# A weighted sum over eight experts: eight tokens per partition and store, weights in one transfer, loads and stores on separate queues

## The chip, the cores and the metric

The kernel runs on one core of a Trainium2 chip. The metric is the device time of one execution in microseconds; the time before is 721.33 us, the median of three runs (721.21 to 722.09). The profile shows one execution with a span of 720.4 us.

## The reference

For each of 16 x 1024 = 16,384 tokens there are eight expert outputs of 512 floats and eight weights. The result is their weighted sum:

```python
batch, seq, n_experts, expert_dim = 16, 1024, 8, 512
weights = combine_weights[..., np.newaxis]
return np.sum(expert_outputs * weights, axis=2).astype(np.float32)
```

All of it is float32. The kernel must read 268.4 MB of expert outputs and 0.5 MB of weights and write 33.6 MB. Each byte that is read takes part in one multiply-add, so no input is used twice.

## The kernel before

The tokens are cut into 64 chunks of 256. Each of the 128 partitions holds J = 2 tokens that follow each other in memory, so a partition's part of a load is one run of 2 x 8 x 512 x 4 B = 32 KB, and the runs of all partitions together are 4 MB in one piece. A chunk's output is 128 runs of 4 KB.

**Loads and queues.** `issue_load(m)` (L52) takes an input tile and a weight tile from pools of four and issues the load of chunk m on the SP queue for even m and on the ACT queue for odd m (L56). The weights of the chunk, 8 KB, come by a separate transfer from the POOL queue (L60). The loads of the last two chunks are cut in two, one token each (L59). Loads are issued three chunks ahead (LA = 3); from chunk 4 on, a load must wait until VectorE is done with the chunk four before it.

**Products.** For each token, VectorE makes the first product with `tensor_scalar_mul` (L77) and then adds seven more, each with one `scalar_tensor_tensor` (L83), which multiplies by a weight and adds to the accumulator `acc`. The chunk's store (L92) goes on the queue that did not load the chunk: ACT for even n, SP for odd n. Output tiles come from a pool of four, so the first product of a chunk waits until the store four chunks earlier has landed.

**The last two chunks.** They are handled together after the loop. ScalarE makes the products of experts 4 to 7 in bf16 (L111), VectorE those of experts 0 to 3 (L116, L122), then VectorE adds the two halves (L130, L135, L138), and each token's half of the output is stored by itself on SP (L141).

**What sets the order.** Each engine's instructions run in the order in which the scheduler put them, and an engine's queue is in order too: a transfer that ACT issues stands among ACT's computing instructions. On ACT the table load and the first product of the tail (L111) stand ahead of the load of chunk 63 (L59).

In the changed kernel the corresponding lines are: loads L62 (whole chunk) and L72 (pieces), the first product L86 on ScalarE, the seven multiply-adds L98, stores L113, and the weights L128.

Of the kernel before, what the change touches and what calls it, by code (L numbers as in the profile page):

```python
# [1 line left out]

# [4 lines left out]


@with_exitstack  # L10
def kernel(
    ctx: ExitStack,
    tc: tile.TileContext,
    expert_outputs: bass.AP,
    combine_weights: bass.AP,
    out: bass.AP,
):
    nc = tc.nc
    fp32 = mybir.dt.float32
    bf16 = mybir.dt.bfloat16  # L20

    B, S, E, D = expert_outputs.shape
    T = B * S
    P = 128
    J = 2
    n_steps = T // (P * J)

    eo_blk = expert_outputs.rearrange("b s e d -> (b s) e d").rearrange(
        "(n p j) e d -> n p j e d", p=P, j=J
    )  # L30
    w_blk = combine_weights.rearrange("b s e -> (b s) e").rearrange(
        "(n p j) e -> n p j e", p=P, j=J
    )
    o_blk = out.rearrange("b s d -> (b s) d").rearrange(
        "(n p j) d -> n p j d", p=P, j=J
    )

    in_pool = ctx.enter_context(tc.tile_pool(name="in_pool", bufs=4))
    w_pool = ctx.enter_context(tc.tile_pool(name="w_pool", bufs=4))
    out_pool = ctx.enter_context(tc.tile_pool(name="out_pool", bufs=4))  # L40
    prod_pool = ctx.enter_context(tc.tile_pool(name="prod_pool", bufs=2))

    ES = E // 2
    K_TAIL = 2

    load_engines = [nc.sync, nc.scalar]

    LA = 3
    in_tiles: list[bass.AP | None] = [None] * n_steps
    w_tiles: list[bass.AP | None] = [None] * n_steps  # L50

    def issue_load(m: int) -> None:  # L52
        in_t = in_pool.tile([P, J, E, D], fp32, name="in_t")
        w_t = w_pool.tile([P, J, E], fp32, name="w_t")
        if m < n_steps - K_TAIL:
            load_engines[m % 2].dma_start(out=in_t, in_=eo_blk[m])  # L56
        else:
            for j in range(J):
                load_engines[m % 2].dma_start(out=in_t[:, j], in_=eo_blk[m, :, j])  # L59
        nc.gpsimd.dma_start(out=w_t, in_=w_blk[m])  # L60
        in_tiles[m] = in_t
        w_tiles[m] = w_t  # L62

    for m in range(min(LA, n_steps)):
        issue_load(m)

    for n in range(n_steps):
        if n + LA < n_steps:
            issue_load(n + LA)
        if n >= n_steps - K_TAIL:  # L70
            continue
        in_tile = in_tiles[n]  # L72
        w_tile = w_tiles[n]
        acc = out_pool.tile([P, J, D], fp32)

        for j in range(J):
            nc.vector.tensor_scalar_mul(  # L77
                out=acc[:, j, :],
                in0=in_tile[:, j, 0, :],
                scalar1=w_tile[:, j, 0:1],  # L80
            )
            for e in range(1, E):
                nc.vector.scalar_tensor_tensor(  # L83
                    out=acc[:, j, :],
                    in0=in_tile[:, j, e, :],
                    scalar=w_tile[:, j, e : e + 1],  # L86
                    in1=acc[:, j, :],
                    op0=mybir.AluOpType.mult,
                    op1=mybir.AluOpType.add,
                )  # L90

        load_engines[(n + 1) % 2].dma_start(out=o_blk[n], in_=acc)  # L92

    tail_steps = list(range(n_steps - K_TAIL, n_steps))
    tail_accs = {}
    tail_prods = {}
    for n in tail_steps:
        acc = out_pool.tile([P, J, D], fp32, name="acc")  # L98
        prods = prod_pool.tile([P, J, E - ES, D], bf16, name="prods")
        tail_accs[n] = acc  # L100
        tail_prods[n] = prods

    for j in range(J):
        for n in tail_steps:
            in_tile = in_tiles[n]
            w_tile = w_tiles[n]
            acc = tail_accs[n]
            prods = tail_prods[n]

            for e in range(ES, E):  # L110
                nc.scalar.mul(  # L111
                    out=prods[:, j, e - ES, :],
                    in_=in_tile[:, j, e, :],  # L113
                    mul=w_tile[:, j, e : e + 1],
                )
            nc.vector.tensor_scalar_mul(  # L116
                out=acc[:, j, :],
                in0=in_tile[:, j, 0, :],
                scalar1=w_tile[:, j, 0:1],
            )  # L120
            for e in range(1, ES):
                nc.vector.scalar_tensor_tensor(  # L122
                    out=acc[:, j, :],
                    in0=in_tile[:, j, e, :],
                    scalar=w_tile[:, j, e : e + 1],
                    in1=acc[:, j, :],
                    op0=mybir.AluOpType.mult,
                    op1=mybir.AluOpType.add,  # L128
                )
            nc.vector.tensor_add(  # L130
                out=prods[:, j, 0:2, :],
                in0=prods[:, j, 0:2, :],
                in1=prods[:, j, 2:4, :],
            )
            nc.vector.tensor_add(  # L135
                out=prods[:, j, 0, :], in0=prods[:, j, 0, :], in1=prods[:, j, 1, :]
            )
            nc.vector.tensor_add(  # L138
                out=acc[:, j, :], in0=acc[:, j, :], in1=prods[:, j, 0, :]
            )  # L140
            nc.sync.dma_start(out=o_blk[n, :, j], in_=acc[:, j, :])  # L141


# [1 line left out]
_INS = ['expert_outputs', 'combine_weights']  # L145
_OUTS = [((16, 1024, 512), 'float32')]


# [23 lines left out]
```

## Time and profile before

| what | value |
|---|---|
| span | 720.4 us |
| VectorE busy | 644.4 us in 1020 instructions |
| of it the multiply-adds, L83 | 868 x 743 ns by the records |
| first products, L77 | 124 x 482 ns |
| ScalarE busy | 11.4 us, all after 690 us |
| moved by the transfers | 302.63 MB, mean 420 GB/s |
| a load of 4 MB, issue to landing | 33.5 us (median) |
| a store of 512 KB, issue to landing | 33.5 us (median) |
| the last store of 256 KB, issue to landing | 3.0 us (median) |

The time of a row in the page is that of its records. Instructions on VectorE overlap a little, so 14 multiply-adds that are recorded at 743 ns each pass in 9.28 us. The time from issue to landing of a load is long because several loads are queued at once; it is not the time that a load takes when it is alone. The DMA rate of a slice is what all 16 transfer engines of the core moved in it.

### The profile page before, as it was taken

How to read it: one execution, taken by the hardware profiler on the slowest of the kernel's cores; microseconds unless marked ns; L12 is line 12 of the kernel's file. 1: busy time of each engine (PE TensorE's matmuls, PEld its weight loads, DVE VectorE, ACT ScalarE, POOL GpSimd, SP SyncE). 2: the span in 40 equal slices, each digit the busy share in tenths (PEclk: the TensorE clock that was granted, in tenths of full speed). 3: DMA queues.
4: the chain of work that ended last, by engine and by line, in shares of the span. 5: the costliest groups of instructions: out<-in, count | busy, mean ns of one | idle time of the engine just before them, and what ended most of it. 6: DMA issues, size and time to landing. Idle time of an engine off the chain costs nothing.

```text
span 720.4 us, 1532 instructions
## 1 busy us (share of the span) xinstructions
DVE 644.4 (89%) x1020; ACT 11.4 (2%) x17; POOL 35.8 (5%) x68
## 2 busy tenths in 40 slices
DVE  0799999999998999989998999989998999999977
ACT  0000000000000000000000000000000000000023
POOL 1000000000000000000000000000000000000000
DMA  9999999999999999999999999999999999999993
GB/s 380 437 416 451 427 426 430 427 424 439 443 431 426 426 423 431 438 436 434 431 423 426 435 430 442 432 424 427 430 429 432 442 431 428 430 425 428 433 359 120
DMA packets 21068, 302.63 MB, mean 420 GB/s; under 512 B 3136, under 2 KB 4160, under 8 KB 12608
## 3 DMA queue, kind: packets, MB, share of 16 engines
q1 hardware_dynamic: 9792, 151.52, 49.2%
q10 hardware_dynamic: 9216, 150.47, 48.9%
q0 software_dynamic: 2048, 0.53, 0.3%
q14 instruction: 12, 0.10, 0.0%
HBM read 268.96 MB, written 33.55 MB: 420 GB/s over the span
## 4 chain that ended last, share of the span: by engine, by line
DMA 63%; DVE 35%; issue 1%; DVEq 0%; SPq 0%
DMA out_dram<-acc 56%; DVE acc L83 30%; DMA in_t<-in_expert_outputs_dram 8%; DVE acc L77 3%; DVE acc L122 1%; DVE acc L138 0%; DVE prods L130 0%; DVE acc L116 0%; DVE prods L135 0%; DVEq L77 0%; DVEq L116 0%; SPq L92 0%
## 5 line engine op out<-in xcount | busy, mean ns | idle before, releaser
L83 DVE SCALAR_TENSOR_TENSOR acc<-in_t,w_t,acc 128x512 f32<-128x512 f32 x868 | 580.1, 743 | 0.0
L77 DVE TENSOR_SCALAR acc<-in_t,w_t 128x512 f32<-128x512 f32 x124 | 54.6, 482 | 66.3 <-DMA in_t<-in_expert_outputs_dram 43.4
L60 POOL DMA_DIRECT2D w_t<-in_combine_weights_dram x64 | 35.6, 556 | 637.7 <-DVE acc L83 636.9
L111 ACT ACT_TABLE_LOAD x1 | 1.3, 1283 | 690.6 <-DMA in_t<-in_expert_outputs_dram 690.6
L111 ACT ACTIVATE prods<-in_t,w_t 128x512 bf16<-128x512 f32 x16 | 10.1, 709 | 9.0 <-DMA in_t<-in_expert_outputs_dram 9.0
L122 DVE SCALAR_TENSOR_TENSOR acc<-in_t,w_t,acc 128x512 f32<-128x512 f32 x12 | 8.9, 745 | 0.0
L116 DVE TENSOR_SCALAR acc<-in_t,w_t 128x512 f32<-128x512 f32 x4 | 1.9, 481 | 5.3 <-DMA out_dram<-acc 5.3
L138 DVE TENSOR_TENSOR acc<-acc,prods 128x512 f32<-128x512 f32 x4 | 2.8, 688 | 0.0
L130 DVE TENSOR_TENSOR prods<-prods 128x1024 bf16<-128x1024 bf16 x4 | 2.7, 683 | 0.0
L135 DVE TENSOR_TENSOR prods<-prods 128x512 bf16<-128x512 bf16 x4 | 1.7, 417 | 0.0
L156 POOL MEMSET const-float32-0.0<- 128x1 f32 x1 | 0.1, 99 | 0.2 <-issue 0.2
L156 POOL MEMSET const-bfloat16-1.0<- 128x1 bf16 x1 | 0.1, 102 | 0.0
L156 POOL MEMSET const-float32-1.0<- 128x1 f32 x1 | 0.1, 99 | 0.0
L156 POOL MEMSET const-uint8-127<- 128x1 uint8 x1 | 0.1, 99 | 0.0
## 6 DMA issues: line engine op xcount, KB each, us to landing
in_t<-in_expert_outputs_dram ACTq DMA_DIRECT2D x31, 4096.0 KB, 33.5
in_t<-in_expert_outputs_dram SPq DMA_DIRECT2D x31, 4096.0 KB, 33.3
out_dram<-acc ACTq DMA_DIRECT2D x31, 512.0 KB, 33.5
out_dram<-acc SPq DMA_DIRECT2D x31, 512.0 KB, 33.4
in_t<-in_expert_outputs_dram SPq DMA_DIRECT2D x2, 2048.0 KB, 31.2
in_t<-in_expert_outputs_dram ACTq DMA_DIRECT2D x2, 2048.0 KB, 13.9
w_t<-in_combine_weights_dram POOLq DMA_DIRECT2D x64, 8.0 KB, 6.9
out_dram<-acc SPq DMA_DIRECT2D x4, 256.0 KB, 3.0
```

Source lines behind the costliest of these rows:

```text
L60: nc.gpsimd.dma_start(out=w_t, in_=w_blk[m])
L77: nc.vector.tensor_scalar_mul(out=acc[:, j, :], in0=in_tile[:, j, 0, :], scalar1=w_tile[:, j, 0:1],)
L83: nc.vector.scalar_tensor_tensor(out=acc[:, j, :], in0=in_tile[:, j, e, :], scalar=w_tile[:, j, e : e + 1], in1=acc[:, j, :], op0=mybir.Al ...
L111: nc.scalar.mul(out=prods[:, j, e - ES, :], in_=in_tile[:, j, e, :], mul=w_tile[:, j, e : e + 1],)
L116: nc.vector.tensor_scalar_mul(out=acc[:, j, :], in0=in_tile[:, j, 0, :], scalar1=w_tile[:, j, 0:1],)
L122: nc.vector.scalar_tensor_tensor(out=acc[:, j, :], in0=in_tile[:, j, e, :], scalar=w_tile[:, j, e : e + 1], in1=acc[:, j, :], op0=mybir.Al ...
L130: nc.vector.tensor_add(out=prods[:, j, 0:2, :], in0=prods[:, j, 0:2, :], in1=prods[:, j, 2:4, :],)
L135: nc.vector.tensor_add(out=prods[:, j, 0, :], in0=prods[:, j, 0, :], in1=prods[:, j, 1, :])
L138: nc.vector.tensor_add(out=acc[:, j, :], in0=acc[:, j, :], in1=prods[:, j, 0, :])
L156: nc = _bacc.Bacc("TRN2", target_bir_lowering=False, num_devices=1)
```

## The change

The kernel is rewritten around the same arithmetic. Eight tokens that follow each other in memory now belong to one partition (K = 8). Loads still carry two tokens per partition (32 KB runs), but the runs of neighbouring partitions now lie 128 KB apart. The accumulator holds eight tokens, and one store writes 2 MB in runs of 16 KB for every four loads. All loads are issued by SP, four chunks ahead, into five buffers; the stores are issued by ACT, but for the last three. The weights of all tokens come in one transfer at the start, issued by ACT, with 16 runs of 256 B for each partition. ScalarE makes the first product of each token and writes it into the accumulator; VectorE adds the other seven. The last seven chunks are loaded in pieces, which get smaller towards the end, so that work on the last data can start before all of it is there. The last stores are smaller, too. The bf16 products of the last two chunks are gone.

The aim is to make the transfers' runs longer and fewer, to take work off VectorE and the POOL queue, to keep loads from standing behind stores or computing instructions, and to shorten the stretch between the last load and the end.

```diff
-    J = 2
-    n_steps = T // (P * J)
+    K = 8
+    G = 8
+    J = 2
+    N = T // (P * K)
...
-    in_pool = ctx.enter_context(tc.tile_pool(name="in_pool", bufs=4))
-    w_pool = ctx.enter_context(tc.tile_pool(name="w_pool", bufs=4))
-    out_pool = ctx.enter_context(tc.tile_pool(name="out_pool", bufs=4))
-    prod_pool = ctx.enter_context(tc.tile_pool(name="prod_pool", bufs=2))
+    in_pool = ctx.enter_context(tc.tile_pool(name="in_pool", bufs=5))
+    w_pool = ctx.enter_context(tc.tile_pool(name="w_pool", bufs=1))
+    out_pool = ctx.enter_context(tc.tile_pool(name="out_pool", bufs=2))
...
+    w_t = w_pool.tile([P, N, K, E], fp32, name="w_t")
+    chunks = [(n, k) for n in range(N) for k in range(0, K, J)]
+    last = len(chunks) - 1
...
+    def load(i):
+        n, k = chunks[i]
+        t = in_pool.tile([P, J, E, D], fp32, name="in_t")
+        in_tiles[i] = t
+        src = x[n, :, k : k + J]
+        if i < last - 6:
+            nc.sync.dma_start(out=t, in_=src)
+            return
+        for j in range(J):
+            if i == last and j == J - 1:
+                cuts = (0, 2, 4, 5, 6, 7, 8)
+            elif i >= last - 2:
+                cuts = (0, 4, 8)
+            else:
+                cuts = (0, 8)
+            for a, b in zip(cuts, cuts[1:]):
+                nc.sync.dma_start(out=t[:, j, a:b], in_=src[:, j, a:b])
...
+    def first(i):
...
+                nc.scalar.mul(
+                    out=acc[:, a + j],
+                    in_=in_tiles[i][:, j, 0],
+                    mul=w_t[:, n, k + j, 0:1],
+                )
...
+    def rest(i):
...
+            for e in range(1, E):
+                nc.vector.scalar_tensor_tensor(
+                    out=acc[:, a + j],
+                    in0=in_tiles[i][:, j, e],
+                    scalar=w_t[:, n, k + j, e : e + 1],
+                    in1=acc[:, a + j],
...
+    def store(i):
...
+        if i < last - 3:
+            if a == G - J:
+                put(nc.scalar, 0, G)
+        elif a == 2:
+            put(nc.scalar, 0, 4)
+        elif a == 4:
+            put(nc.sync, 4, 6)
+        elif a == 6:
+            put(nc.sync, 6, 7)
+            put(nc.sync, 7, 8)
...
+    AHEAD = 4
+    load(0)
+    nc.scalar.dma_start(out=w_t.rearrange("p n k e -> p n (k e)"), in_=w)
+    for i in range(1, AHEAD):
+        load(i)
+    first(0)
+    for i in range(len(chunks)):
+        if i + AHEAD <= last:
+            load(i + AHEAD)
+        if i < last:
+            first(i + 1)
+        rest(i)
+        store(i)
```

More of the change, by code (lines that the diff above doesn't have):

```diff
@@ L19 @@
     fp32 = mybir.dt.float32
-    bf16 = mybir.dt.bfloat16
+    mult, add = mybir.AluOpType.mult, mybir.AluOpType.add
     B, S, E, D = expert_outputs.shape
@@ L24 @@
     P = 128
+    K = 8
+    G = 8
     J = 2
-    n_steps = T // (P * J)
-    eo_blk = expert_outputs.rearrange("b s e d -> (b s) e d").rearrange(
-        "(n p j) e d -> n p j e d", p=P, j=J
-    )
-    w_blk = combine_weights.rearrange("b s e -> (b s) e").rearrange(
-        "(n p j) e -> n p j e", p=P, j=J
-    )
-    o_blk = out.rearrange("b s d -> (b s) d").rearrange(
-        "(n p j) d -> n p j d", p=P, j=J
-    )
-    in_pool = ctx.enter_context(tc.tile_pool(name="in_pool", bufs=4))
-    w_pool = ctx.enter_context(tc.tile_pool(name="w_pool", bufs=4))
@@ L40 @@
-    out_pool = ctx.enter_context(tc.tile_pool(name="out_pool", bufs=4))
-    prod_pool = ctx.enter_context(tc.tile_pool(name="prod_pool", bufs=2))
[L43 to L74, printed above, removed]
-        for j in range(J):
[L77 to L80, printed above, removed]
-            )
+    N = T // (P * K)
@@ new lines @@
+    x = expert_outputs.rearrange("b s e d -> (b s) e d").rearrange(
+        "(n p k) e d -> n p k e d", p=P, k=K
+    )
+    w = combine_weights.rearrange("b s e -> (b s) e").rearrange(
+        "(n p k) e -> p n (k e)", p=P, k=K
+    )
+    o = out.rearrange("b s d -> (b s) d").rearrange("(n p k) d -> n p k d", p=P, k=K)
+    in_pool = ctx.enter_context(tc.tile_pool(name="in_pool", bufs=5))
+    w_pool = ctx.enter_context(tc.tile_pool(name="w_pool", bufs=1))
+    out_pool = ctx.enter_context(tc.tile_pool(name="out_pool", bufs=2))
@@ new lines @@
+    w_t = w_pool.tile([P, N, K, E], fp32, name="w_t")
+    chunks = [(n, k) for n in range(N) for k in range(0, K, J)]
+    last = len(chunks) - 1
+    in_tiles = {}
+    accs = {}
+    pin = tc.keep_in_program_order
+    def load(i):
[6 more added lines that the diff above has]
+            return
+        for j in range(J):
+            if i == last and j == J - 1:
[6 more added lines that the diff above has]
+                nc.sync.dma_start(out=t[:, j, a:b], in_=src[:, j, a:b])
@@ new lines, in acc_of @@
+    def acc_of(i):
+        n, k = chunks[i]
+        g = (n, k // G)
+        if g not in accs:
+            accs[g] = out_pool.tile([P, G, D], fp32, name="acc")
+        return accs[g], k % G
+    def first(i):
+        n, k = chunks[i]
+        acc, a = acc_of(i)
+        for j in range(J):
+            pin(
+                nc.scalar.mul(
[3 more added lines that the diff above has]
+                )
+            )
@@ L82 @@
+    def rest(i):
+        n, k = chunks[i]
+        acc, a = acc_of(i)
+        for j in range(J):
             for e in range(1, E):
                 nc.vector.scalar_tensor_tensor(
[L84 to L89, printed above, removed]
-                )
-        load_engines[(n + 1) % 2].dma_start(out=o_blk[n], in_=acc)
@@ L94 @@
[L94 to L141, printed above, removed]
@@ new lines, in rest, with put @@
+                    out=acc[:, a + j],
+                    in0=in_tiles[i][:, j, e],
+                    scalar=w_t[:, n, k + j, e : e + 1],
+                    in1=acc[:, a + j],
+                    op0=mult,
+                    op1=add,
+                )
+    def store(i):
+        n, k = chunks[i]
+        acc, a = acc_of(i)
+        k0 = k - a
+        def put(queue, lo, hi):
+            pin(queue.dma_start(out=o[n, :, k0 + lo : k0 + hi], in_=acc[:, lo:hi]))
+        if i < last - 3:
[8 more added lines that the diff above has]
+            put(nc.sync, 7, 8)
```

## The prediction

> **What bounds the kernel now.** I read the page's 40 slices first, then the waits, the stretches, and last the end of the timeline. On the page, the rows of busy time, of DMA rate and of queues:
>
> ```profile
> DVE 644.4 (89%) x1020; ACT 11.4 (2%) x17; POOL 35.8 (5%) x68
> ...
> GB/s 380 437 416 451 427 426 430 427 424 439 443 431 426 426 423 431 438 436 434 431 423 426 435 430 442 432 424 427 430 429 432 442 431 428 430 425 428 433 359 120
> ...
> q1 hardware_dynamic: 9792, 151.52, 49.2%
> q10 hardware_dynamic: 9216, 150.47, 48.9%
> ```
>
> VectorE looks busiest, but the rate is flat from the second slice to the 38th, and the shares of the queues sum to 98.4% of all 16 DMA engines. Which of the two paces the other is told by VectorE's waits:
>
> ```profile
> DVE acc L77 <- DMA in_t<-in_expert_outputs_dram: 43.4, 25, 22.9
> DVE acc L77 <- DMA out_dram<-acc: 22.9, 24, 1.9
> ```
>
> 22.9 of the 43.4 us is the first load. The rest are about 1 us each, every chunk from 154 us on: VectorE needs 10.07 us a chunk, the transfers more. The stretches (columns: busy us per engine, clock, DMA share, GB/s) show the same, and where it stops:
>
> ```profile
> 154.00:660.00 506.00, 464.93 (x734) 0.00 (x0) 24.79 (x46) 1.00 1.01 431
> 660.00:689.00 29.00, 26.69 (x44) 0.00 (x0) 1.07 (x2) 1.00 0.98 420
> 689.00:693.00 4.00, 4.00 (x7) 2.42 (x3) 0.00 (x0) 1.00 0.51 155
> 693.00:701.00 8.00, 4.47 (x8) 1.43 (x3) 0.00 (x0) 1.00 1.05 435
> 701.00:706.00 5.00, 3.20 (x6) 4.74 (x8) 0.00 (x0) 1.00 0.85 299
> 706.00:716.00 10.00, 9.97 (x18) 2.83 (x5) 0.00 (x0) 1.00 0.23 87
> ```
>
> So: transfers bound the kernel to 689 us; then a hole, the last 4 MB alone, and ten microseconds of VectorE with the transfers nearly idle. The timeline tells what made the hole:
>
> ```profile
> 690.57 1.28 ACT L111 ACT_TABLE_LOAD   x1 [690.57 <-DMA in_t<-in_expert_outputs_dram]
> 690.72 0.82 ACTq L59 DMA_DIRECT2D in_t<-in_expert_outputs_dram  x2
> ```
>
> The last loads stand on ACT's in-order queue behind the tail's first product, which waits for chunk 62's data. Their buffer had been free since about 673.5 us.
>
> **What the Trainium skill says.** "DMA: Bandwidth & Descriptors", Bandwidth: 16 ports give 435 GB/s. The trace agrees: 431 to 432. Same page, Queues, rings and completion order: each engine takes turns between queues, a packet at a time. The packet records agree: at 300 to 345 us each engine goes row by row, a 32 KB load row of one queue, a 4 KB store row of the other. Same page, Latency and other measured facts: a row pitch of 512 KiB costs copies between HBM tensors 3% (207 against 214 GB/s); no run here shows one.
>
> **The change, part by part.**
> Prices from the packet records (a row on one engine): 32 KB 1213 ns, 16 KB 611, 8 KB 309, 4 KB 159, 2 KB 85, 512 B 27, completion 9. The records overlap: the share is 1.01, and a chunk's records, 8 x (1213 + 159) + 54 = 11.03 us, pass in 10.96 (56 chunks between 52.4 and 666.3 us). So I multiply by 0.9935.
>
> 1. *Stores of 16 KB rows, no weight packets per chunk.* Per chunk now 8 x 1213 + 2 x 611 + 11 = 10.94 us recorded, x 0.9935 = 10.87, against 10.96: 0.09 x 64 = 6 us less, all on the path.
> 2. *Loads on one queue.* Between 684 and 689 us one queue alone carried 430 to 432 GB/s, so one is enough. Five buffers keep 4 loads queued; a VectorE chunk (below) is shorter than a load, so buffers come free in time. Cost nothing.
> 3. *First product on ScalarE.* 128 VectorE instructions go. 14 multiply-adds pass in 9.28 us, 0.663 each: 896 x 0.663 = 594 us, 9.3 a chunk. ScalarE adds 2 x 0.71 us a chunk (row L111, which writes bf16; at twice that it would still hide), beside VectorE. Both hide under 10.87. On ACT's queue a 2 MB store stands behind the next chunk's product and so waits for that chunk's load, some 2 us; its buffer is wanted 4 chunks later. The store waits at L77 (22.9 us) go, but that is time VectorE had to spare.
> 4. *Tail.* The loads stay on SP, so the hole of about 3 us goes. Transfers to the last landing: loads 57 x 8 x 1213 + 8 x 8 x 611 + 10 x 8 x 309 + 2 x 8 x 159 + 4 x 8 x 85 ns = 622.1 us; stores but for the last 1 MB, 15 x 8 x 611 + 8 x 309 = 75.8; weights 2.3 (step 5); completions 0.9. Sum 701.1, x 0.9935 = 696.6. Before, two loads (19.3 us) and the first weights were in at 22.3, so the start costs 2.6: 699.2. One engine lags: near 666 us the last of a load's 16 completions comes 6.8 us after the first, the 15th only 0.8. That engine also carries the 8 KB instruction fetches (queue q14; 11 by then), 0.6 us each. With some 1130 instructions instead of 1532 I take 8 to 9: 5.2 us. **Last landing: 704.4.** The last token's final seven multiply-adds start after the token before: its second half lands 4.8 us before the end (2 MB at 431), seen 0.6 later, 4 x 0.663, then 7 x 0.663: VectorE ends 3.1 after the last landing. Before, VectorE ended at 716.05 and the span at 720.4: 4.35 for store and end. 704.4 + 3.1 + 4.35 = 711.9; the median lay 0.9 above the span: **712.8 us**.
> 5. *Weights in one transfer on ACT's queue.* 2048 runs of 256 B, 128 an engine. Trace of before: no such rows. A row's records fit 8.4 ns plus its bytes at 27.2 GB/s: 18 ns each, 2.3 us; upper end 60 ns (7.7 us), from the 85 of a 2 KB row. The cost is not the work but the turn. Behind it on ACT's queue: the table load (1.28 us) and the first product, which all of VectorE waits for. If one packet holds 16 runs, as the 4 KB that a partition receives, the weights need 8 turns beside load rows, some 12 us, in by 16: VectorE starts near 18, frees its first buffer near 27, and the five loads issued at once last to 51. Nothing lost.
>
> **The rivals.**
> *A: no stall, as summed, 712.8.*
> *B: a packet is one run.* Then each run waits for a 32 KB row: the five loads (40 rows an engine, 48 us) pass with only 40 of 128 runs, to 51.5. The other 88 take 1.6 to 5.3 us, then 1 of completion, 1.3 table load, 0.8 product, 9.3 VectorE for chunk 0, and 1.2 from issue to the first packet: transfers resume at 66.7 to 70.4. Idle beyond the runs' own time: 13.6 to 17.3 us. **728 us**, slower than before. For it: the 2 KB store rows at L141 are separate records, and the turns go strictly row by row. Against: queue q0's weight packets hold eight 64 B rows each (512 B), so a packet of several runs exists here; and the page names 9 to 17 descriptors a packet as typical. Five or more runs a packet are enough to escape.
> *C: the new pitch hurts.* Rows of a load now lie 128 KB apart instead of 32. At 1 to 3% of the transfers, 7 to 21 us: **720 to 734**. Against: the pitch is a quarter of the one that cost 3%.
> *D: the slow engine's lag vanishes* or records overlap more: 5 us less, **708**.
>
> **How the numbers follow.** A 61%, B 26%, C 6%, D 7%. The likeliest is A, 712.8. The range reaches from 709 (A with half the lag) to 730, which takes in B, and leaves out about 8% below and 8% above. Faster by over 0.2% (below 719.9): A, D and a little of C, 0.69. Within it: 0.04, from C. Slower: B and most of C, 0.27.
>
> **What would show it.** Steps 1 and 2: a rate of 432 to 433 in the middle and 10.9 us between chunks. Step 3: VectorE busy about 665 us by its records (896 x 743 ns), waiting for loads, never for stores. Step 4: no hole after 680, VectorE done some 3 us after the last load. Step 5: VectorE's first instruction near 18 us; B shows it past 55, with an idle slice near 55 to 67. C shows 32 KB rows over 1213 ns. The forecast is wrong if the weights land after about 38 us, or if the rate is under 428.

## The result, and the profile after

The changed kernel takes 733.06 us (median of four, 732.67 to 733.57) against 721.68 for the kernel before (four executions beside it), a ratio of 1.016 with a 95% interval of 1.0145 to 1.0174: 1.6% slower. The forecast was 712.8, with a range up to 730. Rival B told the mechanism; its 728 is 5 us short, because it stood on the same 712.8.

From the page of the changed kernel, the busy times, the 40 slices, ACT's queue (packets, MB, share) and the weights' transfer (last column: us from issue to landing):

```profile
DVE 603.8 (83%) x896; ACT 86.9 (12%) x129; POOL 0.2 (0%) x4
...
DVE  0009999999997969887897978969888897989998
...
DMA  9994999999999999999999999999999999999993
GB/s 381 429 366 190 400 420 430 432 432 431 436 429 435 431 431 430 436 436 420 440 426 438 430 432 431 435 429 434 432 434 426 438 431 433 424 429 429 425 416 142
...
q10 hardware_dynamic: 4368, 33.03, 10.7%
...
w_t<-in_combine_weights_dram ACTq DMA_DIRECT2D x1, 512.0 KB, 53.1
```

VectorE has three empty slices at the start (18.3 us each), and the transfers are weak in the fourth. The weights, 0.5 MB, need 53 us. The timeline of the start shows what hangs on them:

```profile
0.73 0.46 ACTq L128 DMA_DIRECT2D w_t<-in_combine_weights_dram  x1
...
12.94 1.28 ACT L86 ACT_TABLE_LOAD   x1 [12.94 <-DMA in_t<-in_expert_outputs_dram]
53.87 6.23 ACT L86 ACTIVATE acc<-in_t,w_t 128x512 f32<-128x512 f32 x10 [39.65 <-DMA w_t<-in_combine_weights_dram]
54.62 55.74 DVE L98 SCALAR_TENSOR_TENSOR acc<-in_t,w_t,acc 128x512 f32<-128x512 f32 x84 [54.62 <-ACT acc L86]
```

ScalarE waits 39.65 us for the weights, then makes ten products at once, because five chunks are there; VectorE's first instruction is at 54.6. The stretches (length; busy us of VectorE, ScalarE and POOL with their instructions; clock; DMA share; GB/s) tell what the transfers do meanwhile:

```profile
20.00:50.00 30.00, 0.00 (x0) 0.00 (x0) 0.00 (x0) 1.00 0.99 423
50.00:70.00 20.00, 15.38 (x24) 6.23 (x10) 0.00 (x0) 1.00 0.42 149
...
400.00:650.00 250.00, 213.12 (x320) 31.40 (x47) 0.00 (x0) 1.00 1.00 431
```

Up to 50 us they run at full rate and fill the five buffers. Then they have nowhere to put data until VectorE has used chunk 0. The packet records, each the time of one packet on one DMA engine, give the cause row by row: from 3.4 to 51.5 us each DMA engine does one 256 B run of the weights, one 32 KB load row, one run, and so on. I call this taking turns. At about 51.5 the load rows end; some 43 of an engine's 128 runs have passed, and the other 85 pass in less than 2 us, 14 to 25 ns apart. The next load row comes at about 65.

The middle is as fast as it was (431 GB/s). The end shows no hole. There VectorE is at work without a gap, so it no longer waits for loads (timeline of VectorE alone, the last 70 us):

```profile
658.11 70.20 DVE L98 SCALAR_TENSOR_TENSOR acc<-in_t,w_t,acc 128x512 f32<-128x512 f32 x93 [1.36 <-ACT acc L86]
```

93 instructions in 70.2 us are 0.755 each. In the middle they come 0.663 apart.

### The profile page after: what moved, and what is told of

It is laid out like the page before. It is cut to its first block, busy times and chain, and to the rows that moved or that the text cites. A ratio compares the mean times of both kernels' runs of the same rounds, so it can differ in the third digit from the quotient of the medians.

```text
span 731.4 us, 1345 instructions
## 1 busy us (share of the span) xinstructions
DVE 603.8 (83%) x896; ACT 86.9 (12%) x129; POOL 0.2 (0%) x4
## 3 DMA queue, kind: packets, MB, share of 16 engines
q10 hardware_dynamic: 4368, 33.03, 10.7%
## 4 chain that ended last, share of the span: by engine, by line
DMA 62%; DVE 29%; another core or an unknown queue 5%; issue 2%; ACT 1%; SPq 0%; ACTq 0%; DVEq 0%
DMA in_t<-in_expert_outputs_dram 62%; DVE acc L98 29%; ACT acc L86 1%; ACT L86 0%; SPq L72 0%; ACTq L86 0%; SPq L62 0%; DVEq L98 0%
## 5 line engine op out<-in xcount | busy, mean ns | idle before, releaser
L98 DVE SCALAR_TENSOR_TENSOR acc<-in_t,w_t,acc 128x512 f32<-128x512 f32 x896 | 603.8, 746 | 124.5 <-ACT acc L86 122.0
L86 ACT ACTIVATE acc<-in_t,w_t 128x512 f32<-128x512 f32 x128 | 85.6, 714 | 620.9 <-DMA in_t<-in_expert_outputs_dram 528.8
L86 ACT ACT_TABLE_LOAD x1 | 1.3, 1283 | 12.9 <-DMA in_t<-in_expert_outputs_dram 12.9
## 6 DMA issues: line engine op xcount, KB each, us to landing
w_t<-in_combine_weights_dram ACTq DMA_DIRECT2D x1, 512.0 KB, 53.1
```

Of the source, the lines that this page charges most:

```text
L86: nc.scalar.mul(out=acc[:, a + j], in_=in_tiles[i][:, j, 0], mul=w_t[:, n, k + j, 0:1],)
L98: nc.vector.scalar_tensor_tensor(out=acc[:, a + j], in0=in_tiles[i][:, j, e], scalar=w_t[:, n, k + j, e : e + 1], in1=acc[:, a + j], op0=mult,
```

## The experiments

Each time below is the median of 4 to 17 executions, which lie 0.2 to 2.2 us apart from lowest to highest. The ratio is to the kernel before, run beside it, with its 95% interval in brackets.

**The weights first.** The same transfer on the loads' queue, ahead of them:

```diff
-    load(0)
-    nc.scalar.dma_start(out=w_t.rearrange("p n k e -> p n (k e)"), in_=w)
+    nc.sync.dma_start(out=w_t.rearrange("p n k e -> p n (k e)"), in_=w)
+    load(0)
```

> The changed kernel with the same weight transfer issued on SP ahead of the first load, in place of ACT behind it; nothing else. Theory 1 (each 256 B run on ACT's queue waits its turn behind a 32 KB load row): ahead of the loads in one queue there are no turns, the 128 runs of an engine take 2.3 us (18 ns each), the weights land before 8 us, VectorE starts near 16 us, no idle slice near 53 to 65; 14 us less than the changed kernel, 718 to 721 us. Rival (the transfer of 2048 runs is slow by itself, some 50 us): the loads now stand behind it and the time rises above 760 us.

Measured: 719.05 us, ratio to the kernel before 0.9962 (0.9948 to 0.9977). The same 2048 runs now land 4.2 us after their issue. VectorE's start in the timeline:

```profile
17.60 22.61 DVE L98 SCALAR_TENSOR_TENSOR acc<-in_t,w_t,acc 128x512 f32<-128x512 f32 x34 [17.60 <-ACT acc L86]
```

14.0 us are gone with one moved line. The transfer is not slow by itself. This edit changes its queue and its place at once; the next two runs tell what made it slow.

**The weights from POOL.** The changed kernel with `nc.gpsimd` in place of `nc.scalar` in that line.

> The changed kernel with the weight transfer issued by POOL at the same place, behind the first load's issue; nothing else. Theory 1, that the number of packets counts and not the runs: queue q0 packed eight 64 B runs in a packet before; if it packs runs of 256 B too, an engine has 8 to 64 packets instead of 128, the weights land between 12 and 40 us, and with 8 to 28 packets the stall is gone: 719 to 721 us. If it sends one run a packet, the weights land near 53 us again and the time is 733 us. Rival (any transfer of this shape takes some 50 us beside loads): 733 us in every case.

Measured: 719.07 us, ratio 0.9964 (0.9951 to 0.9977). The page's queues, and the issue with its us to landing:

```profile
q10 hardware_dynamic: 2304, 32.51, 10.6%
q0 software_dynamic: 144, 0.52, 0.2%
...
w_t<-in_combine_weights_dram POOLq DMA_DIRECT2D x1, 512.0 KB, 17.7
```

Queue q0 carries the whole transfer in 128 packets of 4096 B and 16 completions: 16 runs a packet, eight packets an engine, each still with its turn beside a load row. ACT's queue had sent 2048 packets of 256 B (q10 falls from 4368 to 2304: 2048 runs and 16 completions). The weights are in at 18.9 us, and the time is that of the run with the weights first. So the packet counts, not the run, and the two queues pack differently.

**Three buffers.** The changed kernel, stall and all, with fewer loads issued at once.

```diff
-    in_pool = ctx.enter_context(tc.tile_pool(name="in_pool", bufs=5))
+    in_pool = ctx.enter_context(tc.tile_pool(name="in_pool", bufs=3))
...
-    AHEAD = 4
+    AHEAD = 2
```

> The changed kernel with three input buffers and loads two chunks ahead in place of five and four; the weight transfer stays on ACT behind the first load. Theory 1 (the runs take turns with whatever load rows are queued, and pass freely once the queue is empty): three loads are issued at once, 24 rows an engine, so the weights land near 2.6 + 29.3 + 2 = 34 us instead of 53, VectorE starts near 35, and the idle stretch of the transfers is as long as before, from about 34 to 46 us; the time stays at 731 to 735 us. Rival (the weights' landing near 53 is a property of their transfer): VectorE starts at 54 again, the transfers idle from 32 us, and the time rises to 750 us or more.

Measured: 732.9 us, ratio 1.0155 (1.0138 to 1.0171). VectorE's start, from the timeline, and one of the stretches:

```profile
35.23 35.20 DVE L98 SCALAR_TENSOR_TENSOR acc<-in_t,w_t,acc 128x512 f32<-128x512 f32 x53 [35.23 <-ACT acc L86]
```

```profile
34.00:46.00 12.00, 10.77 (x17) 3.78 (x6) 0.00 (x0) 1.00 0.13 38
```

The weights land when the queued load rows are through, here 24 an engine, at 34 us. From the last of the weights to the next load row it is 11.7 us, as in the changed kernel, and the time is the same. So the landing follows the number of load rows queued beside the weights, and the loss is what follows the landing (first product, chunk 0, the next issue).

**VectorE's order in the tail.** The multiply-adds of chunks 57 to 62 go in turns between the two tokens, as the scheduler has them in the middle; where loads are cut by token, it had put each token's seven in a row.

```diff
+        if last - 6 <= i < last:
+            pairs = [(j, e) for e in range(1, E) for j in range(J)]
```

> The changed kernel, with the multiply-adds of the chunks 57 to 62 in turns between the two tokens, as the scheduler has them in the chunks before; chunk 63 and all transfers unchanged, the weight stall stays. Theory 2 (in the tail each multiply-add waits for the one just before it on the same accumulator and takes 0.787 us instead of 0.663, so VectorE is the bound of the tail): spacing 0.66 us in these chunks, a chunk in 9.3 instead of 10.8 us, VectorE waits for loads again, 2 to 5 us less, 728 to 731 us. Rival (the last loads set the end, and VectorE's spacing is beside them): within 0.7 us of 733.1.

Measured: 732.9 us, ratio 1.0162 (1.0144 to 1.0179). No gain, the rival's number. The spacing did fall from 0.787 to 0.663 us, but in this order each chunk's second instruction waits for its second token.

**Both edits.**

> Both edits together: weights on SP ahead of the first load, and the chunks 57 to 62 in turns between the two tokens. If the two faults are independent, the gains add: 733.1 - 14 - 2 to 5, 714 to 717 us, near the 712.8 that was forecast without a stall. Rival (the tail's cost is only what the stall left behind): no less than the kernel with the weights first alone.

Measured: 719.27 us, ratio 0.9968 (0.9956 to 0.9979), the same as with the weights first alone. Missed again. VectorE waits for the second token of chunk 62 and then has 27 instructions left:

```profile
695.57 18.73 DVE L101 SCALAR_TENSOR_TENSOR acc<-in_t,w_t,acc 128x512 f32<-128x512 f32 x27 [0.58 <-ACT acc L86]
```

The last loads landed some 6 us later than forecast; the next run takes away a store that stands beside them.

**The last big store out of the loads' way.** With the weights first, the 1 MB store of chunks 60 and 61 moves to SP, behind all loads:

```diff
         elif a == 2:
-            put(nc.scalar, 0, 4)
+            put(nc.sync, 0, 4)
```

> Weights first (as in the run of that name), and the 1 MB store of chunks 60 and 61 on SP, where it stands behind all loads, instead of ACT, where its 8 KB rows take turns with the last loads. Theory 3 (the last landing on the slowest engine sets the end, and every store row that gets its turn before it moves it back): 1 MB less ahead of the last load, 2.4 us at 431 GB/s; VectorE ends 1.5 to 2.4 us earlier, 716.5 to 717.5 us. Rival (VectorE's chain of the last chunks, back to back from 640 us on, sets the end): within 0.7 us of 719.05.

Measured: 718.88 us, ratio 0.9961 (0.9947 to 0.9975). The last token's product started at 703.4 us, for 706.2 with the weights first alone, but VectorE had been busy without a gap and ended as late as ever:

```profile
643.94 70.20 DVE L98 SCALAR_TENSOR_TENSOR acc<-in_t,w_t,acc 128x512 f32<-128x512 f32 x93 [1.35 <-ACT acc L86]
```

The same 93 instructions, the same 70.20 us as in the changed kernel: moving loads forward does nothing for them.

**Both tail edits, with the weights first.**

> Weights first, the multiply-adds of chunks 57 to 62 in turns between the two tokens, and the 1 MB store of chunks 60 and 61 on SP behind the loads. Theory 5 (the tail has two limits of the same length: VectorE's chain at 0.787 us an instruction, and the last loads that share turns with store rows; taking away one alone leaves the other): both gone, the last loads land 2 to 3 us earlier and VectorE is free to follow, 714 to 716.5 us. Rival (something else sets the end, such as the lag of one DMA engine): within 0.7 us of 719.

Measured: 718.64 us, ratio 0.9962 (0.995 to 0.9975). Missed: VectorE was free of its chain, but the same 27 instructions stand at the end:

```profile
696.78 18.72 DVE L101 SCALAR_TENSOR_TENSOR acc<-in_t,w_t,acc 128x512 f32<-128x512 f32 x27 [0.57 <-ACT acc L86]
```

In this order chunk 62 can begin in earnest only when its second token is there. Its 13 remaining instructions and the 14 of chunk 63 then need until 715.5 (the profiled execution is the slowest of the five, 720.36 us). So this edit did not take VectorE's limit away; it put another one of VectorE in its place. A further run was to put the second token's first instructions of the last chunk between the first token's:

> As the run with turns and stores, and in the last chunk too the second token's first multiply-adds stand between those of the first token. Theory 5: VectorE has some 1 us less to do after the last landing, 0.5 to 1.5 us less than that run. Rival (VectorE waits for the last pieces, not for itself): no difference above 0.4 us.

Measured: 719.03 us, ratio 0.9964 (0.9951 to 0.9976). The scheduler already had the last chunk in that order (the waits of the last 16 instructions are the same in both traces), so this is the same instruction order twice. It shows that 0.4 us between two medians here mean nothing.

**Tokens in a pipeline.** As with both tail edits, but from chunk 60 on a token's last three multiply-adds stand between the first four of the next, across chunks.

```diff
+        for j in range(J):
+            old = left.pop() if left else None
+            for e in range(1, 5):
+                step(i, j, e)
+                if old and e < 4:
+                    step(*old, e + 4)
+            left.append((i, j))
```

> As the run with turns and stores (718.64), but in chunks 60 to 63 the last three multiply-adds of a token stand between the first four of the next token, across chunks: no instruction waits for the one just before it, and none waits for a token that it does not need. Theory 6 (VectorE sets the end of the tail, by its order: chained it needs 5.4 us a token where a token lands every 4.9, and in turns inside a chunk it starts only at the chunk's second token): VectorE ends some 7 us after the last token's first piece instead of 10.8, 2 to 3.5 us less, 715 to 716.5 us. Rival (the lag of the DMA engine with VectorE's fetches sets the end whatever the order): within 0.7 us of 718.6.

Measured: 717.96 us, ratio 0.9944 (0.9931 to 0.9958), the lowest median of the complete kernels. It gained 0.7 us where 2 to 3.5 were expected, which by the medians is the rival's result. The timeline speaks for the order all the same:

```profile
701.79 11.73 DVE L98 SCALAR_TENSOR_TENSOR acc<-in_t,w_t,acc 128x512 f32<-128x512 f32 x17 [0.24 <-ACT acc L86]
```

VectorE ends 8.8 us after the last token's product starts, for 10.8 with both tail edits, if not the 7 expected. The product starts at 704.7 in both profiled executions, and these took 718.35 and 720.36 us, 2.0 apart. Five executions of each leave open whether the gain is nearer to 0.7 or to 2.

**Less work on VectorE.** As with the last stores on SP, but two of the seven multiply-adds are left out in chunks 57 to 63, so the output lacks two products there.

```diff
-            for e in range(1, E):
+            for e in range(1, E if i < last - 6 else E - 2):
```

> As the run with the last stores on SP (718.88), with the multiply-adds of experts 6 and 7 left out in chunks 57 to 63 (2 of 7 for 14 tokens a partition; the output lacks them), all transfers unchanged. Theory 6: five chained multiply-adds take 3.9 us a token, less than the 4.9 in which a token lands, so VectorE follows the loads and the end is the last landing, near 707, plus 1 to 3 us and the last store: 711 to 714 us. Rival (the loads or the lag set the end): within 0.7 us of 718.9.

Measured: 714.63 us, ratio 0.9907 (0.9894 to 0.9921), 4.25 less than the run it builds on; the expected 711 to 714 was missed by 0.6. VectorE waits between tokens now:

```profile
690.16 3.90 DVE L98 SCALAR_TENSOR_TENSOR acc<-in_t,w_t,acc 128x512 f32<-128x512 f32 x5 [0.52 <-ACT acc L86]
695.13 3.90 DVE L98 SCALAR_TENSOR_TENSOR acc<-in_t,w_t,acc 128x512 f32<-128x512 f32 x5 [1.07 <-ACT acc L86]
700.10 7.71 DVE L98 SCALAR_TENSOR_TENSOR acc<-in_t,w_t,acc 128x512 f32<-128x512 f32 x10 [1.07 <-ACT acc L86]
```

With the transfers unchanged and less work, the end moves: VectorE's work bounded the tail. Seven chained instructions need 5.4 us a token where one lands every 4.9 to 5.0; five need 3.9. VectorE itself ends 6.3 us earlier, at 707.8; the last store now lands 4.0 us after its issue instead of 2.0, with the three stores ahead of it landing at 709.3 to 711.2.

**The lagging DMA engine.** Two kernels with instructions that nobody waits for. With the weights first, 1024 memsets on POOL:

> Weights first, and 1024 memsets of one element a partition on POOL, which has nothing else to do; nobody waits for them. Theory 4 (each 8 KB instruction fetch costs one DMA engine about 0.96 us, 0.31 for itself and 0.65 more on the row behind it, and the lagging engine sets every landing): 1024 instructions of 64 B are 8 more fetches, all on the same engine, the lag near 640 us grows from 7 to about 15 us, and the time rises by 6 to 8 us to 725 to 727 us. Rival (the lag is hidden by what the other engines do, or the fetches spread): within 0.7 us of 719.05.

Measured: 718.80 us, ratio 0.9959 (0.9944 to 0.9974). Eight more fetches are in the records, but the time did not move. In the spread of a load's 16 completions near 514 us, the last is 5.3 us behind the first and the 15th 5.1; without the memsets it is 5.2 and 1.5. So a second engine seems to lag beside the first one, and no further than it. Which engine carries which fetch the records do not name; this spread is the evidence.

Then 512 memsets on VectorE, added to the kernel with both tail edits:

> As the run with turns and stores, and 512 memsets of one element a partition on VectorE, near the start, where VectorE has time to spare later on; nobody waits for them. Theory 4b (POOL's fetches fell on another DMA engine than VectorE's, and the end is set by the engine that carries VectorE's fetches, some 0.9 us each): 4 more fetches on that engine, its lag near 640 us grows by 3 to 4 us, and the time by 2.5 to 4 us. Rival (the lag is hidden): within 0.7 us of the run with turns and stores.

Measured: 722.72 us, ratio 1.0017 (1.001 to 1.0024), 4.1 us more than the run it builds on (3.1 between the two profiled executions). The page has 14 fetches for 10:

```profile
q14 instruction: 14, 0.11, 0.0%
```

Near 534 us the last completion is 10.6 us behind the first instead of 7.4 (6.2 with the weights first alone), while the first one comes at the same time, 534.0 for 534.2. Four more fetches on one engine: 3.2 us of lag by then against the run it builds on. The memsets' own time on VectorE is not the cause: the first multiply-add starts at 18.8 us in both, and from 20 to 160 us the stretches show 425 to 432 GB/s, against 419 to 434 without memsets.

**The kernel before, without its hole.** Only the loads of chunk 63 change:

```diff
-                load_engines[m % 2].dma_start(out=in_t[:, j], in_=eo_blk[m, :, j])
+                nc.sync.dma_start(out=in_t[:, j], in_=eo_blk[m, :, j])
```

> The kernel before with one edit: the two loads of chunk 63 go on SP instead of ACT, so they no longer stand behind the tail's table load and first product. If the hole at 689 to 693 us cost the time that its length says, they are issued near 674 us instead of 690.7, the hole closes and the time falls by 2 to 4 us, to 718 to 719.5 us. Rival (the ten microseconds of VectorE work at the end set the time whenever the loads land): within 0.7 us of 721.6.

Measured: 720.9 us, ratio 0.9991 (0.9983 to 1.0). The rival was right: 0.6 us, inside its band. The stretches of this kernel:

```profile
689.00:693.00 4.00, 4.00 (x7) 2.46 (x3) 0.00 (x0) 1.00 1.05 448
...
706.00:716.00 10.00, 9.43 (x17) 2.56 (x4) 0.00 (x0) 1.00 0.17 66
```

The hole is filled (share 1.05 for 0.51), and VectorE still needs its ten microseconds at the end.

**A larger pitch.** With the weights first, a partition owns 128 tokens in a row, so that load rows lie 2 MB apart. The stores' rows lie 256 KB apart instead of 16, and a partition's weights are one run of 4 KB.

```diff
-        "(n p k) e d -> n p k e d", p=P, k=K
+        "(p n k) e d -> n p k e d", p=P, n=N, k=K
```

> Weights first, with the tokens dealt so that a partition owns 128 tokens in a row: load rows of 32 KB lie 2 MB apart instead of 128 KB, and a partition's weights are one run of 4 KB; everything else the same. If the pitch costs nothing in loads from HBM to SBUF (what the 128 KB pitch showed, 1213 ns a row), the time is within 1 us of 719.05. Rival C (large pitches slow the rows, as the skill states for copies between HBM tensors, 164 against 214 GB/s at 2 MiB): rows of 1500 ns or more, 800 us or more.

Measured: 744.53 us, ratio 1.0318 (1.0302 to 1.0334), 25.5 us more than with the 128 KB pitch. Neither number fits. The stretches, first of this kernel, then of the one with the weights first:

```profile
160.00:640.00 480.00, 403.30 (x604) 57.61 (x87) 0.00 (x0) 1.00 1.00 425
640.00:700.00 60.00, 52.45 (x73) 6.50 (x9) 0.00 (x0) 1.00 1.00 380
700.00:720.00 20.00, 14.32 (x20) 2.16 (x3) 0.00 (x0) 1.00 0.99 260
```

```profile
160.00:640.00 480.00, 410.04 (x614) 58.09 (x87) 0.00 (x0) 1.00 1.00 432
640.00:690.00 50.00, 47.03 (x65) 6.50 (x9) 0.00 (x0) 1.00 1.01 426
690.00:700.00 10.00, 9.68 (x15) 1.45 (x2) 0.00 (x0) 1.00 1.02 418
```

In the stretch of 32 KB rows the rate falls by 1.6%, some 10 of the 25.5 us (an estimate, from 57 loads of 10.92 us); the tail has the rest. The mean record of a load row of 32 KB is 1241 ns against 1219, of 16 KB 643 against 614, of 8 KB 452 against 313, of 4 KB 213 against 163. The 16 KB store rows take 611 ns in both, so it is the loads that suffer. Why, no run here shows.

## Why the prediction was wrong, point by point

**Step 5, the weights: the step that failed.** The likeliest case rested on a packet of several runs. On ACT's queue a packet was one run of 256 B, and the weights landed at 53.9 us, past the 38 that I had set as the mark of a wrong forecast. The two signs that I set against each other were both true, of different queues: q0's packets hold several runs because POOL's transfers are packed so (the page "DMA: Bandwidth & Descriptors" of the Trainium skill, section SWDGE vs HWDGE vs iDMA, states packets of preferably up to 4096 B for them; the POOL run shows exactly 4096), and L141's 2 KB rows on SP's queue had each been a record of its own. The weights were moved to a queue of the second kind, and the sign from that kind should have had the larger chance. The 9 to 17 descriptors a packet that the same page calls typical (section Queues, rings and completion order) do not hold for ACT's queue here. Rival B's working held: five loads through by 51.5, as forecast; landing at 53.9 against 54 to 58; load rows again at 65 against 66.7 to 70.4. The loss was 14.0 us against 13.6 to 17.3, at the low end because the runs pass 14 to 25 ns apart and because the table load was not in the chain: it ran at 12.9 us, long before.

**The other 6 us: the forecast without a stall.** With the weights first the time is 719.05, not 712.8. The terms:

- *Step 1, rate.* The first completion of a load comes every 10.92 us (32 loads from 197.6 to 546.9 in the changed kernel), against 10.96 before and 10.87 forecast: half the gain, some 3 us. Two small things are in it. The factor 0.9935 came from a kernel in which two load queues alternate; here the 10.96 us recorded for a chunk pass in 10.92, a factor of 0.996. And a 32 KB row takes 1216 ns on average between 160 and 640 us, where it took 1213 before; whether the lone queue or the pitch of 128 KB does that, no run separates.
- *Step 4, lag of one engine.* 5.2 us forecast, 7.0 in the changed kernel near 600 us and 6.2 with the weights first. The fetch at 261 us in the changed kernel takes 0.31 us and lengthens the row behind it from 1213 to 1862 ns, so 0.96 in all, where I had 0.6; for two of the fetches it is 0.7. One to 2 us. In the run with memsets on VectorE 3.2 us more lag made the profiled execution 3.1 us longer, so this engine's lag reaches the end in full.
- *Step 4, last landing.* The pieces of the tail move at 418 to 426 GB/s where I had 431: 1 us more over the last 60. Together these three take the last landing from 704.4 to 709 or 710; the packet records of the run with the weights first have it at 710.5.
- *Step 4, VectorE after it.* I priced the last instructions at 0.663 us and let VectorE start each token as it landed. But 0.663 is the spacing of two tokens in turns; in a row on one accumulator it is 0.787, and the cut loads made the scheduler put them in a row. VectorE was behind the loads from 644 us on and ended at 714.5 instead of 707.5. The run with less work shows that this bounds the tail. Against it, the store and the end cost 3.1 us where I had 4.35.
- *From span to time.* I added 0.9 us; it is about 1.75 in every execution that lists both (719.35 us for a span of 717.6, 733.14 for 731.4). I had set the span of a slower execution against a median: the kernel before takes 722.2 us where its span is 720.4.

As a sum the terms close: the last landing 6.1 us late, VectorE 0.9 later behind it, the end 1.25 shorter, 0.85 from span to time, together 6.6 us, and the profiled execution took 719.35. But undoing one does not give back its share: the last landing and VectorE's chain end close together. Moving the landing forward alone gained nothing (718.88), because VectorE's chain stayed. The turns gained nothing with either place of the store (719.27, 718.64 and 719.03), because VectorE then had its 27 instructions left after the second token of chunk 62. Only less work on VectorE moved the end clearly.

**Steps 2 and 3 held** in the main. One queue carries 431 to 432 GB/s, though part of step 1's shortfall may be its cost. In the middle VectorE waits for ScalarE's first product, which waits for a load; nothing there waits for a store. My sign for step 3, 665 us busy, was misread: the busy row counts overlapping records once, 603.8 us.

**The hole of the kernel before** did not cost what its length says, as the run without it shows; the forecast summed the tail anew and did not lean on it.

**Rivals C and D.** C, 1 to 3% of the transfers, fell for this change: at the 128 KB pitch the mean 32 KB row takes 1216 ns against 1213, 0.2%, and the middle runs at 431 to 432 GB/s. The median, on which my price of 1213 ns rests, would not have shown it: it is 1213 even at the 2 MB pitch, where the mean is 1238 in the same stretch. D fell, too: the lag grew.

## What to carry to other kernels

Beside large loads, a transfer of many short runs waits one load row for each packet, however few bytes it has: put what everything waits for ahead of the loads in their own queue, or issue it where runs are packed, and see how many packets the queue made of it. Longer runs should help, too, but were not tried beside loads here. In a tail where two limits end together, an edit that frees one side shows nothing; leave out work on one side to see which holds. Reordering work is no such test, since a new order brings its own waits. Price an instruction at the spacing it has in its own order, since instructions in turns between two accumulators and instructions in a row on one do not take the same time.

## What the runs showed of the hardware

- The same 2048 runs of 256 B went as 2048 packets from ACT's queue and as 128 packets of 4096 B from POOL's; beside 32 KB load rows they landed after 53.1 and 17.7 us, and ahead of the loads in SP's queue after 4.2 us.
- A multiply-add of 128x512 floats that needs the result of the one just before it follows after 0.787 us; with another accumulator's in between they come 0.663 us apart.
- Each instruction fetch of 8 KB delays one DMA engine by 0.7 to 1 us in the records of the changed kernel, and a load is complete only when its last engine is: four more fetches for VectorE cost 4.1 us, eight more for POOL nothing.
- At a row pitch of 2 MB, loads of 32 KB rows lose 1.6% and a tail of smaller rows falls to 260 GB/s, 25.5 us in all. The page "DMA: Bandwidth & Descriptors" of the Trainium skill, section Latency and other measured facts, has 164 against 214 GB/s for copies between HBM tensors with 16 KB rows at that pitch; for loads into SBUF the loss measured here is far smaller, 1.6% with 32 KB rows and 5% in the mean record of 16 KB rows.
